# A macaron block with RWKV7 and window attention: attention scores in one plain product each, and four smaller moves of work

## The chip, the cores and the metric

The kernel runs on one core of one Trainium2 chip. The metric is the device time of one execution in microseconds (us), measured in three runs; the median counts. One further execution was recorded by the hardware profiler, and the rows below are from that one.

## The reference, cut to what matters

All arrays are float32; batch 1, 512 rows of 1024 channels, hidden width 2816. Decay, gates and the details of the RWKV7 recurrence are left out here.

```python
h = rms_norm(x, norm_ffn1);  x = x + 0.5 * swiglu(h, gate1, up1, down1)
h = rms_norm(x, norm_mix);   p = h @ w_in            # RWKV columns, and q, k, v of the attention
q, k, v = split(p_attn)                              # 8 query heads, 2 key heads, 64 channels each
o_rwkv = rwkv7_time_mix(p_rwkv)                      # a recurrence over the rows
scores = einsum('bnqhgd,bnkhd->bnhgqk', qb, kb) / 8  # blocks of 128 rows against this and the last block
probs  = softmax(where(band, scores, -inf), with one sink per head)
o_attn = einsum('bnhgqk,bnkhd->bnqhgd', probs, vb)
x = x + concat(o_rwkv, o_attn) @ w_out
h = rms_norm(x, norm_ffn2);  x = x + 0.5 * swiglu(h, gate2, up2, down2)
return rms_norm(x, norm_final)
```

## The kernel before, in words

**Stages.** Feed-forward block a, the projections by w_in, the mixer (RWKV7 and attention together), the product by w_out, feed-forward block b, the last norm. Each large product is done in three passes (mm3w, L681 to L685): both operands are split into a high part that TensorE reads in one pass and the low rest, and high by high, low by high and high by low are summed. ScalarE (ACT) makes the high part of the weights (L160, `hi...`), VectorE (DVE) the low part (L169, `lo...`). The weights come in through SyncE's queue (SP) and GpSimd's (POOL).

**The start.** `start` loads x in two halves of its columns, four tiles of 128 rows each, and the weights of the first pieces, all from SP's queue. Then each row tile's half is turned on TensorE (`start_turn`, `xta`, L536), multiplied by the norm's gain on DVE (`xga`), and split (`AaM`, `AaP`). Turns 0 and 1 come ahead of the first products, turns 2 and 3 inside them, at t = 1 of `plain_step`.

**The feed-forward blocks.** The hidden columns are cut into pieces, which a loop over q takes in order. The first four (`plain_step`) compute 256 hidden columns with plain products into the banks `Pa`, `Pb`; at the end ACT applies Silu (L658, `gta`), DVE multiplies (L659, `gta` again), and for each of four row tiles a `hidden_turn` (TensorE transposes L731 `hta`, ACT copies L732 `hTa`) is put on the list `due` with the q at which it is issued. After that come the pieces of a seven-product scheme (banks X, Y, Q; twelve matmuls each per row pair), whose operands DVE and ACT form and split between them (L547 to L573).

**The mixer.** The RWKV7 part runs over 8 chunks of 64 rows; each is a chain of short steps over all heads (`z` products `pz`, `zd` ACT's copy L1322, `u` products `pu` L1328, state updates `pS`, output). Attention is cut in 8 units, u = 2n + h for query block n and key head h: scores (`sc`), maximum and mask on DVE, exponential on ACT, transposes `pT`, product by V (`av`). A table of step names, ORDER, sets by hand the order in which all of these are issued, so that attention fills TensorE while a chain step is on ACT or DVE. What comes ahead of it, `join` with `beside`, inverts small triangular matrices for RWKV (`px`, `py`, copies `TT`, L1110) while the last projection (`in_ps_av`, attention's v) runs.

**Scores.** Units 0 and 1 (query block 0) use plain float32 products of 64 rows by 128 columns (L1468). For the six others k is split once into `ks` and `kl` (`split_k`) and q by block into `qs` (`split_q`), on ACT and DVE, all of it issued in `beside(0)`; each of four heads j then takes two matmuls of 256 columns, L1471 and L1472.

**The end.** `last_row` scales a row tile by its norm: ACT makes the half k = 0 (L871), DVE the half k = 1 (L873), and SP issues both stores (L874).

Of the kernel before, what the change touches and what calls it, by code (L numbers as in the profile page):

```python
# [5 lines left out]
F32 = mybir.dt.float32  # L6
F32R = mybir.dt.float32r
AF = mybir.ActivationFunctionType
ALU = mybir.AluOpType
AX = mybir.AxisListType  # L10
P = 128
S = 512
# [4 lines left out]
C = 64  # L17
NC = S // C
# [23 lines left out]
OUTW = 4  # L42
# [11 lines left out]
gb.0 ud.2 s.2 w.4.1 m.6.0 o.2 a.2 n.2.0 oe.2 v.3 ah.2 we.4 te.3 n.2.1 z.3 m.6.1 wa.4.0 b.4 ve.3 al.2 sc.5 wd.4.1 zd.3  # L54
w.6.0 u.3 m.5.0 a.3 w.6.1 uv.3 t.4 m.5.1 ah.3 ud.3 s.3 we.6 te.4 al.3 o.3 n.3.0 sc.7 w.5.0 n.3.1 z.4 wa.6.0 m.7.0 b.5
w.5.1 wd.6.1 a.4 m.7.1 zd.4 t.6 oe.3 we.5 ah.4 wd.5.1 w.7.0 u.4 al.4 bp.1 uv.4 te.6 g.1 wd.5.0 w.7.1 bo.1 t.5 ud.4
we.7 s.4 wd.7.0 te.5 o.4 wd.7.1 a.6 oe.4 n.4.0 ge.1 a.5 n.4.1 ah.6 q.1 t.7 al.6 ah.5 b.6 wh.0 gb.1 z.5 al.5 te.7 var.1 ux
wl.0 q.0 a.7 zd.5 var.0 u.5 ah.7 wo.1.0 wh.1 al.7 uv.5 ns.1 s.5 ud.5 wl.1 ht.1 o.5 wo.1.1 n.5.0 oe.5 q.2 n.5.1 z.6 mg.1
b.7 wo.3.0 zd.6 var.2 xa.1 u.6 ns.0 wo.3.1 uv.6 ns.2 ud.6 s.6 xa.3 mh.1 o.6 n.6.0 ht.0 oe.6 ht.2 n.6.1 wo.0.0 mg.2 z.7
mg.0 mh.2 wo.0.1 zd.7 ml.2 mh.0 u.7 ml.1 wh.2 wo.2.0 xa.0 ud.7 wl.2 o.7 wo.2.1 oe.7 ml.0 q.3 wo.5.0 var.3 wh.3 xa.2  # L60
wl.3 wo.5.1 wo.4.0 xa.5 ns.3 wo.7.0 ht.3 wo.4.1 mg.3 wo.7.1 wh.4 xa.4 mh.3 wl.4 wo.6.0 ml.3 wo.6.1 xa.7 xa.6
# [4 lines left out]
KEEP = "rgvaVOe"  # L66
# [116 lines left out]
class Net:  # L183
# [152 lines left out]
    def start(self, x):  # L336

        nc = self.nc
        self.warm()
        self.consts()  # L340
        xin = self.xin = self.new_rows()
        def load(h, *ts):
            for t in ts:
                nc.sync.dma_start(xin[t][:, h * S:h * S + S], x[0, t * P:(t + 1) * P, h * S:h * S + S])
        a = self.a = self.stream("a")
        load(0, 0)
        a.loads(1)
        load(0, 1, 2, 3)
        a.loads(2)
        load(1, 0, 1, 2, 3)  # L350
        a.loads(4)
        self.first_gain()
        self.ss = self.small("ss_a", 8, "ss")
        self.operands_begin("a")
        for t in range(2):
            self.start_turn(t, 0)
            if t == 0:
                a.split(0)

    def start_turn(self, t, h):  # L360
        self.operand_turn(self.xin[t], t, h, self.gain1)
# [61 lines left out]
    def want_high(self, i):  # L423

        name, srcs = self.plan.pop(0)
        raw, n = self.weights_load(name, srcs)
        hi, lo = (self.wp.tile([P, 8, P], F32R, tag="o" + x, name=f"{x}_{name}", bufs=OUTW) for x in ("hi", "lo"))
        self.nc.scalar.activation(hi, raw, AF.Copy)
        self.half = name, raw, hi, lo

    def want_low(self, i):
        name, raw, hi, lo = self.half
# [13 lines left out]
    def weights(self, name, srcs):  # L446

        raw, n = self.weights_load(name, srcs)
        if name.startswith("be"):
            hi, lo = (self.tile4(f"{c}_{name}", (P, 8, P), F32R) for c in ("hi", "lo"))  # L450
        else:
            if name[0] == "o":
                hi, lo = (self.wp.tile([P, 8, P], F32R, tag="o" + x, name=f"{x}_{name}", bufs=OUTW) for x in ("hi", "lo"))
            else:
                hi, lo = (r.next(P) for r in self.split_rings)
        return self.weights_split(raw, n, hi, lo)
# [178 lines left out]
    def plain_step(self, st, pc):  # L635

        nc = self.nc
        if pc.idx == 0:
            self.banks["P"] = [self.acc(f"P{st.tag}{t}") for t in range(4)]
        bh, bl = st.parts[pc.q]  # L640
        for t in range(4):
            if pc.idx == 0 and t == 1 and st.tag == "a":
                for u in (2, 3):
                    self.operand_turn(self.xin[u], u, 0, self.gain1)
                for u in (2, 3):
                    self.operand_split(P_OPERANDS[1][0], u % 2)
            if pc.idx == 0 and t == 2 and st.tag == "b":
                self.out_turn(7)
            hi, lo = self.A[P_OPERANDS[t // 2][pc.idx // 2]]
            ts = slice(t % 2 * P, t % 2 * P + P)  # L650
            for j in range(2):
                k = 2 * (pc.idx % 2) + j
                self.mm3w(self.banks["P"][t], hi[:, k, ts], lo[:, k, ts], bh[:, j], bl[:, j], pc.idx == 0 and j == 0, pc.idx == 3 and j == 1)
        if pc.idx == 3:
            for t, b in enumerate(self.banks.pop("P")):
                ms = self.ms[:, t:t + 1]
                g, h = self.gt(f"pg{st.tag}{t}")[:, :256], self.gt(f"ph{st.tag}{t}")[:, :256]
                nc.scalar.activation(g, b[:, 256:], AF.Silu, scale=ms)  # L658
                nc.vector.scalar_tensor_tensor(h, b[:, :256], ms, g, ALU.mult, ALU.mult)  # L659
                self.due.append((pc.q + 1 + t, lambda t=t, h=h: self.hidden_turn(st, 5, t, h, 256)))  # L660

    def gu_step(self, st, pc):
        nc = self.nc
# [201 lines left out]
    def last_row(self, t):  # L865
        nc = self.nc
        z, o = self.z[t], self.fs[t][:, 2:3]
        for k in range(2):
            hs = slice(k * S, (k + 1) * S)
            if k == 0:  # L870
                nc.scalar.activation(z[:, hs], z[:, hs], AF.Copy, scale=o)  # L871
            else:
                nc.vector.scalar_tensor_tensor(z[:, hs], self.xN[t][:, hs], o, self.nf[:, hs], ALU.mult, ALU.mult)  # L873
            nc.sync.dma_start(self.out[0, t * P:(t + 1) * P, hs], z[:, hs])  # L874

    def finish(self):
        self.last_row(3)
# [138 lines left out]
    def prep(self, p):  # L1016
        nc = self.nc
        k, r, a, Pd, Pi = self.kT[p], self.rT[p], self.icl[p], self.Pd[p], self.Pi[p]
        c3 = lambda t: t.rearrange("p (c t) -> p c t", c=NC)
        KR = self.KR[p] = self.tile4(f"KR{p}", (P, NC, 2, C))  # L1020
        BK = self.BK[p] = self.tile4(f"BK{p}", (P, NC, 2, C))
        STo = self.STo[p] = self.tile4(f"STo{p}", (P, NC, 2, C))
        kk = self.tile2(f"kk{p}")
        kk3 = c3(kk)
        nc.vector.scalar_tensor_tensor(kk, k, self.v("rwkv_k_k", p), self.knb[p].rearrange("p t s -> p (t s)"), ALU.mult, ALU.mult)
# [133 lines left out]
    def gate(self, p):  # L1159

        nc = self.nc
        if p // 2 not in self.g:
            self.g[p // 2] = self.tile4(f"g{p // 2}")
        pt = self.gps[p] = self.psum(f"g_ps{p}")
        nc.tensor.matmul(pt, self.g2[:, p * P:(p + 1) * P], self.gl, start=True, stop=True)

# [7 lines left out]
    def mixer(self):  # L1174
        nc = self.nc
# [54 lines left out]
        with self.tc.manual_schedule(engines=MAN):  # L1230
# [5 lines left out]
            def beside(i):  # L1236
                if i == 0:
                    part(0, 4)
                    self.split_k()
                    for n in range(1, 4):  # L1240
                        self.split_q(n)
                elif i == 1:
                    self.scores_all(0)
                    part(4, 8)
# [176 lines left out]
    def attn_begin(self):  # L1421
        nc = self.nc
        self.amix = self.pairs("am")
        self.sc, self.qs, self.PT, self.pp = {}, {}, {}, {}

    def attn_values(self):
        self.avn = self.psum("avn", (P, 4, P))
# [4 lines left out]
        self.Vn = self.keep("V", "Vn").rearrange("p (n c) -> p n c", n=4)  # L1432
        self.nc.scalar.activation(self.Vn, self.avn, AF.Copy)

    def split_k(self):

        nc = self.nc
        self.ks = self.x4.tile([P, 2, S], F32R, tag="ks", name="ks", bufs=1)
        self.kl = self.tile2("kl", dt=F32R) if "a" not in KEEP else self.t4.tile([P, 2, S], F32R, tag="kl", name="kl", bufs=1)[:, 0]
        for h in range(2):  # L1440
            r, o = (slice(x * 64, x * 64 + 64) for x in (h, 1 - h))
            nc.scalar.activation(self.ks[r, h], self.k[r], AF.Copy)
            nc.vector.tensor_tensor(self.kl[r], self.k[r], self.ks[r, h].bitcast(F32), ALU.subtract)
            nc.gpsimd.dma_start(self.ks[o, h], self.ks[r, h])

    def split_q(self, n):

        nc = self.nc
        qs = self.qs[n] = self.wp.tile([P, 2, 4, P], F32R, tag="qs", name=f"qs{n}", bufs=3)
        for i in range(2):  # L1450
            js = slice(2 * i, 2 * i + 2)
            for h in range(2):
                r, o = (slice(x * 64, x * 64 + 64) for x in (h, 1 - h))
                q, hi = self.q[i][r, :, n * P:(n + 1) * P], qs[r, h, js]
                nc.scalar.activation(hi, q, AF.Copy)
                nc.vector.tensor_tensor(qs[o, h, js], q, hi.bitcast(F32), ALU.subtract)

    def scores(self, u):
        nc = self.nc
        n, h = u // 2, u % 2  # L1460
        r0 = h * 64
        k0 = 0 if n > 0 else P
        W = 2 * P - k0
        pss = self.psum2(f"sc{u}", (P, 4, 2 * P))
        for j in range(4):
            ks = slice((n - 1) * P + k0, (n + 1) * P)
            if n == 0:
                nc.tensor.matmul(pss[:, j, :W], self.q[j // 2][r0:r0 + 64, j % 2, :P], self.k[r0:r0 + 64, ks], start=True, stop=True)  # L1468
            else:
                q = self.qs[n][:, h, j]  # L1470
                nc.tensor.matmul(pss[:, j, :W], q, self.ks[:, h, ks], start=True, stop=False)  # L1471
                nc.tensor.matmul(pss[:, j, :W], q[r0:r0 + 64], self.kl[r0:r0 + 64, ks], start=False, stop=True)  # L1472
        self.sc[u] = (self.extra4("sc", f"scs{u}", (P, 4, 2 * P)), W, pss) + tuple(self.small(f"{x}{u}", 4, x) for x in ("m", "nm", "es", "den"))

    def scores_max(self, u, half):
# [178 lines left out]
```

## Time and profile before

| | us |
|---|---|
| runs | 999.86, 1001.09, 1001.99 (median 1001.09) |
| the profiled execution's own time | 1002.43 |
| its span, first to last instruction | 1000.7 |
| TensorE busy | 976.9 (98%) |
| VectorE busy | 651.7 (65%) |
| ScalarE busy | 502.9 (50%) |
| mean granted clock of TensorE | 0.988 |

The span is 1.73 us shorter than the execution; that rest lies outside what the profile records. A granted clock of 1.00 is 2.4 GHz, 0.50 is 1.2 GHz. Matmuls are recorded with an overlap, so what a step takes is the distance between the starts of two neighbours rather than the duration of one. A float32 product of the plain kind leaves two matmul records, a pass of a split product one. "Unit" below is one of the attention's eight.

### The profile page before, as it was taken

The numbers are of one execution on the slowest core, as the hardware profiler recorded it, in microseconds if no ns is written. First come the engines' busy times: TensorE is split into PE (matmuls) and PEld (weight loads), VectorE is DVE, ScalarE is ACT, GpSimd is POOL, SyncE is SP. The second block draws the span as 40 slices with busy tenths as digits, with TensorE's granted clock in tenths as the row PEclk, the third lists the DMA queues.
The fourth block names the chain that finished last, engine by engine and source line by source line (L and its number), as shares of the span: only waits on it lengthen the run. The fifth ranks groups of instructions, "written<-read, shape, count | busy, mean of one in ns | idle before, by whom it ended". The sixth has DMA issues, their size and how long they took to land.

```text
span 1000.7 us, 12967 instructions
## 1 busy us (share of the span) xinstructions
PE 976.9 (98%) x5041; PEld 794.6 (79%) x5041; DVE 651.7 (65%) x926; ACT 502.9 (50%) x777; POOL 88.5 (9%) x97
## 2 busy tenths in 40 slices
PE   8799999999999999999989999999999999999996
PEld 6688888888888886788876777887888888888885
DVE  5677667677522548699985687668767668753422
ACT  4655546546521327755466664265554654652302
POOL 0110010110000001120010030101010111000001
PEclk9899999999999999999999899999999999999999
DMA  9474855945332044223110253655594584533202
GB/s 316 106 168 113 225 135 122 232 105 182 111 104 84 12 103 140 75 74 73 43 33 23 52 152 132 226 156 147 124 234 110 143 202 97 206 126 115 75 1 84
DMA packets 83621, 124.09 MB, mean 124 GB/s; under 512 B 12772, under 2 KB 33320, under 8 KB 83560
## 3 DMA queue, kind: packets, MB, share of 16 engines
q1 hardware_dynamic: 67048, 89.17, 27.7%
q0 software_dynamic: 13856, 31.46, 15.8%
q10 hardware_dynamic: 2656, 2.63, 0.9%
q8 instruction: 39, 0.64, 0.3%
q14 instruction: 22, 0.18, 0.1%
HBM read 114.60 MB, written 6.29 MB: 121 GB/s over the span
## 4 chain that ended last, share of the span: by engine, by line
PE 85%; DVE 6%; ACT 4%; issue 2%; DMA 1%; POOL 1%; SPq 0%; POOLq 0%; ACTq 0%; DVEq 0%
PE da L685 4%; PE da L683 4%; PE db L685 4%; PE db L683 4%; PE da L684 4%; PE db L684 4%; PE Xa L685 4%; PE Xa L683 4%; PE Xa L684 4%; PE Xb L685 3%; PE Xb L683 3%; PE Xb L684 3%; PE Qb L685 2%; PE Qa L685 2%; PE Qa L683 2%
## 5 line engine op out<-in xcount | busy, mean ns | idle before, releaser
L160 ACT ACTIVATE hib<-rawa1b 128x1024 fp32r<-128x1024 f32 x38 | 40.2, 1057 | 58.4 <-PE db L684 19.4
L683 PE MATMUL da<-hia,dda 128*128 128x512 f32 x176 | 69.3, 394 | 0.0
L683 PE MATMUL db<-hib,ddb 128*128 128x512 f32 x176 | 68.8, 391 | 0.0
L685 PE MATMUL da<-loa,dda 128*128 128x512 f32 x176 | 68.6, 390 | 0.0
L684 PE MATMUL da<-hia,dda 128*128 128x512 f32 x176 | 68.5, 389 | 0.0
L685 PE MATMUL db<-lob,ddb 128*128 128x512 f32 x176 | 68.5, 389 | 0.0
L684 PE MATMUL db<-hib,ddb 128*128 128x512 f32 x176 | 68.5, 389 | 0.0
L160 ACT ACTIVATE hia<-rawa1a 128x1024 fp32r<-128x1024 f32 x38 | 40.1, 1055 | 49.6 <-DMA rawa1a<-in_ffn_gate_dram 17.6
L169 DVE TENSOR_TENSOR lob<-rawa1b,hib 128x1024 fp32r<-128x1024 f32 x38 | 46.4, 1220 | 28.3 <-PE db L685 22.6
L169 DVE TENSOR_TENSOR lob<-rawa0b,hib 128x1024 fp32r<-128x1024 f32 x38 | 46.4, 1220 | 28.3 <-PE db L685 21.7
L683 PE MATMUL Xa<-hia,AaM 128*128 128x512 f32 x160 | 64.0, 400 | 0.0
L685 PE MATMUL Xa<-loa,AaM 128*128 128x512 f32 x160 | 63.1, 395 | 0.9 <-DVE loa L169 0.9
L685 PE MATMUL Xb<-lob,AbM 128*128 128x512 f32 x160 | 62.6, 392 | 1.3 <-DVE lob L169 1.3
L683 PE MATMUL Xb<-hib,AbM 128*128 128x512 f32 x160 | 63.2, 395 | 0.0
L684 PE MATMUL Xa<-hia,AaM 128*128 128x512 f32 x160 | 62.8, 393 | 0.0
L684 PE MATMUL Xb<-hib,AbM 128*128 128x512 f32 x160 | 62.3, 390 | 0.0
L169 DVE TENSOR_TENSOR loa<-rawa0a,hia 128x1024 fp32r<-128x1024 f32 x38 | 46.4, 1220 | 20.9 <-PE da L685 14.6
L169 DVE TENSOR_TENSOR loa<-rawa1a,hia 128x1024 fp32r<-128x1024 f32 x38 | 46.4, 1220 | 15.8 <-PE da L685 8.8
L160 ACT ACTIVATE hib<-rawa0b 128x1024 fp32r<-128x1024 f32 x38 | 40.1, 1057 | 24.5 <-PE db L684 12.1
L160 ACT ACTIVATE hia<-rawa0a 128x1024 fp32r<-128x1024 f32 x38 | 40.1, 1055 | 15.4 <-PE da L684 11.2
L685 PEld LDWEIGHTS da<-loa,dda 128*128 128x128 f32 x176 | 33.0, 188 | 7.0
L685 PEld LDWEIGHTS db<-lob,ddb 128*128 128x128 f32 x176 | 33.0, 188 | 6.9
(460 smaller groups left out, 2527.9 us busy)
## 6 DMA issues: line engine op xcount, KB each, us to landing
rawa0a<-in_w_in_dram SPq DMA_DIRECT2D x16, 512.0 KB
rawa0a<-in_ffn_down_dram SPq DMA_DIRECT2D x11, 512.0 KB
rawa1a<-in_ffn_down_dram SPq DMA_DIRECT2D x11, 512.0 KB
rawa0b<-in_ffn_down_dram SPq DMA_DIRECT2D x11, 512.0 KB
rawa1b<-in_ffn_down_dram SPq DMA_DIRECT2D x11, 512.0 KB
rawba<-in_ffn_up_dram SPq DMA_DIRECT2D x10, 512.0 KB
rawba<-in_ffn_gate_dram SPq DMA_DIRECT2D x10, 512.0 KB
rawa0a<-in_ffn_gate_dram POOLq DMA_DIRECT2D x10, 512.0 KB, 5.9
```

The costliest lines, as they stand in the source:

```text
L160: self.nc.scalar.activation(hi, raw, AF.Copy)
L169: self.nc.vector.tensor_tensor(lo, raw, hi.bitcast(F32), ALU.subtract)
L683: mm(ps, ah, bh, start=first, stop=False, skip_group_check=True)
L684: mm(ps, al, bh, start=False, stop=False, skip_group_check=True)
L685: mm(ps, ah, bl, start=False, stop=last, skip_group_check=True)
```

## The change

It has five parts. (1) The scores of units 2 to 7 become one plain float32 product per head, 64 rows by 256 columns, as units 0 and 1 have with 128; `split_k` and `split_q` go, with 14 ACT copies, 14 DVE subtractions and two DMAs on POOL. (2) At the start, the first piece's weights are issued by ACT, x follows on SP without them, and turn 1 comes behind the first three products. (3) The four hidden turns of the plain pieces come one step of the loop later in both blocks. (4) The stores of the half k = 0 are issued by ACT. (5) The four loads `ux` (POOL, x from its spill) come behind one norm step, `var.0`. Beside these some tiles share one allocation (`KS`, `g`, `ow`), and the g and h of the plain pieces are taken four by four.

```diff
-we.7 s.4 wd.7.0 ... z.5 al.5 te.7 var.1 ux
-wl.0 q.0 a.7 zd.5 var.0 u.5 ah.7 ...
+we.7 s.4 wd.7.0 ... z.5 al.5 te.7 var.1
+wl.0 q.0 a.7 zd.5 var.0 ux u.5 ah.7 ...
         load(0, 0)
-        a.loads(1)
+        a.loads(1, nc.scalar)
         load(0, 1, 2, 3)
...
-        for t in range(2):
-            self.start_turn(t, 0)
-            if t == 0:
-                a.split(0)
+        self.start_turn(0, 0)
+        a.split(0)
...
                 self.mm3w(self.banks["P"][t], hi[:, k, ts], ...)
+                if st.tag == "a" and (pc.idx, t, j) == (0, 0, 0):
+                    self.start_turn(1, 0)
         if pc.idx == 3:
+            g4, h4 = ([self.gt(f"p{x}{st.tag}{t}")[:, :256] for t in range(4)] for x in "gh")
...
-                self.due.append((pc.q + 1 + t, lambda t=t, h=h: self.hidden_turn(st, 5, t, h, 256)))
+                self.due.append((pc.q + 2 + t, lambda t=t, h=h: self.hidden_turn(st, 5, t, h, 256)))
...
-            nc.sync.dma_start(self.out[0, t * P:(t + 1) * P, hs], z[:, hs])
+            (nc.sync if k else nc.scalar).dma_start(self.out[0, t * P:(t + 1) * P, hs], z[:, hs])
...
                 if i == 0:
                     part(0, 4)
-                    self.split_k()
-                    for n in range(1, 4):
-                        self.split_q(n)
...
-            if n == 0:
-                nc.tensor.matmul(pss[:, j, :W], self.q[j // 2][r0:r0 + 64, j % 2, :P], self.k[r0:r0 + 64, ks], start=True, stop=True)
-            else:
-                q = self.qs[n][:, h, j]
-                nc.tensor.matmul(pss[:, j, :W], q, self.ks[:, h, ks], start=True, stop=False)
-                nc.tensor.matmul(pss[:, j, :W], q[r0:r0 + 64], self.kl[r0:r0 + 64, ks], start=False, stop=True)
+            nc.tensor.matmul(pss[:, j, :W], self.q[j // 2][r0:r0 + 64, j % 2, n * P:(n + 1) * P], self.k[r0:r0 + 64, ks], start=True, stop=True)
```

How the order moves, at three places. First TensorE at the start of the program (`xta` are turns of x, `Pa` the bank of the first products); before, then now:

```order
16 L536 MATMUL xta_139<-pack_106,xN_113 128x128 x4
17 L536 MATMUL xta_152<-pack_106,xN_113 128x128 x4
18 L683 MATMUL Pa_170<-hia,AaM_145 128x512
19 L684 MATMUL Pa_170<-hia,AaM_145 128x512
20 L685 MATMUL Pa_170<-loa,AaM_145 128x512
21 L683 MATMUL Pa_170<-hia,AaM_145 128x512
```

```order
16 L538 MATMUL xta_139<-pack_106,xN_113 128x128 x4
17 L688 MATMUL Pa_162<-hia,AaM_145 128x512
18 L689 MATMUL Pa_162<-hia,AaM_145 128x512
19 L690 MATMUL Pa_162<-loa,AaM_145 128x512
20 L538 MATMUL xta_169<-pack_106,xN_113 128x128 x4
21 L688 MATMUL Pa_162<-hia,AaM_145 128x512
```

The second turn of x stood ahead of the first product and stands behind the third.

Next ScalarE where the mixer begins (`ks`, `qs` are the split k and q, `TT<-px` a copy for the small inverses, `held<-in_ps_av` attention's v, `scs` the first exponentials, `pack<-pz` the first chain step's copy); before, then now:

```order
341 L1110 ACTIVATE held<-py 128x256
342 L1442 ACTIVATE ks<-held 64x512 x2
343 L1455 ACTIVATE qs_3684<-q_2361 64x256 x2
...
348 L1455 ACTIVATE qs_3702<-q_2362 64x256 x2
349 L1110 ACTIVATE TT<-px 32x2x8x32 x2
350 L924 ACTIVATE held<-in_ps_av,pack_106 128x512
351 L1491 ACTIVATE scs_3781,den_3785<-scs_3781,nm_3783 128x128 x4
352 L1493 ACTIVATE es_3784<-es_3784 128x4
353 L1322 ACTIVATE pack<-pz_3809 64x256 x2
```

```order
343 L1115 ACTIVATE held<-py 128x256
344 L1115 ACTIVATE TT<-px 32x2x8x32 x2
345 L929 ACTIVATE held<-in_ps_av,pack_106 128x512
346 L1466 ACTIVATE scs_3742,den_3746<-scs_3742,nm_3744 128x128 x4
347 L1468 ACTIVATE es_3745<-es_3745 128x4
348 L1325 ACTIVATE pack<-pz_3770 64x256 x2
```

Fourteen copies are gone from between the copy of `py` and that of `px`.

Last TensorE at the scores of unit 2 in the mixer (`sc`), between a product by V (`av`) and RWKV's next values (`pv`); before, then now:

```order
2072 L1544 MATMUL av_3893<-PT_3874,held 64x256 x2
2073 L1471 MATMUL sc_3898<-ks,qs_3684 128x256
2074 L1472 MATMUL sc_3898<-kl,qs_3684 128x256
2075 L1471 MATMUL sc_3898<-ks,qs_3684 128x256
2076 L1472 MATMUL sc_3898<-kl,qs_3684 128x256
2077 L1471 MATMUL sc_3898<-ks,qs_3684 128x256
2078 L1472 MATMUL sc_3898<-kl,qs_3684 128x256
2079 L1471 MATMUL sc_3898<-ks,qs_3684 128x256
2080 L1472 MATMUL sc_3898<-kl,qs_3684 128x256
2081 L1280 MATMUL pv_3919<-pack,held 128x128 x4
```

```order
2068 L1519 MATMUL av_3854<-PT_3835,held 64x256 x2
2069 L1447 MATMUL sc_3859<-held,q_2361 128x256 x2
2070 L1447 MATMUL sc_3859<-held,q_2362 128x256 x2
2071 L1283 MATMUL pv_3876<-pack,held 128x128 x4
2072 L1320 MATMUL pz_3883<-SU_3578,KS_2831 128x64 x2
```

Eight matmuls of one pass each have become four plain ones of the same 256 columns, in the same place.

## Rows read from the trace of the kernel before

**Rows 1.** TensorE's waits: engine, what waited for what, total us, times, longest.

```profile
PE hta L731 <- DVE gta L659: 4.6, 1, 4.6
PE avn L1429 <- ACT held L924: 1.4, 1, 1.4
PE pu L1328 <- ACT pack L1322: 0.6, 1, 0.6
```

**Rows 2.** Timeline where the mixer begins: start, us, instruction, idle before.

```profile
511.67 1.29 PE L1134 MATMUL px<-TB,held 32*32 32x32 f32 x128 [1.26 <-ACT held L1110]
...
512.94 5.26 ACT L1455 ACTIVATE qs<-q 64x256 fp32r<-64x256 f32 x12
...
516.61 0.39 PE L508 MATMUL in_ps_av<-h_m,loa 128*128 128x512 f32 x1
...
518.22 1.19 ACT L1110 ACTIVATE TT<-px 32x512 f32<-32x512 f32 x2
...
518.34 0.39 PE L1317 MATMUL pz<-SU,STo 128*128 128x64 f32 x2
...
519.43 0.69 ACT L924 ACTIVATE held<-in_ps_av,pack 128x512 f32<-128x512 f32 x1
...
521.97 0.76 ACT L1322 ACTIVATE pack<-pz 64x256 f32<-64x256 f32 x2
```

**Rows 3.** Timeline of TensorE, scores and products like them.

```profile
530.60 0.38 PE L1471 MATMUL sc<-ks,qs 128*128 128x256 f32 x1
...
533.09 1.16 PE L1280 MATMUL pv<-pack,held 128*128 128x128 f32 x8
...
557.05 1.03 PE L1544 MATMUL av<-PT,held 128*64 128x256 f32 x6
558.01 1.16 PE L1280 MATMUL pv<-pack,held 128*128 128x128 f32 x8
559.00 0.33 PE L1317 MATMUL pz<-SU,KR 128*128 128x64 f32 x2
```

**Rows 4.** Stretches: window, us, engines' busy time (x), TensorE's clock, DMA share, GB/s.

```profile
522.20:529.00 6.80, 6.53 (x27) 3.72 (x28) 4.02 (x17) 3.70 (x11) 0.00 (x0) 0.50 0.01 2
...
563.10:566.50 3.40, 3.40 (x27) 2.05 (x27) 2.94 (x13) 1.05 (x6) 0.00 (x0) 0.51 0.00 0
...
573.40:576.80 3.40, 3.40 (x16) 2.16 (x15) 1.96 (x8) 2.68 (x8) 0.00 (x0) 0.50 0.98 308
...
995.90:998.90 3.00, 0.00 (x0) 0.00 (x0) 0.75 (x1) 0.72 (x1) 0.00 (x0) 0.62 0.93 348
```

**Rows 5.** Timeline of TensorE: eight transposes and their neighbours, at either clock.

```profile
544.82 1.04 PE L1523 MATMUL pT<-pack,scs 128*128 128x128 f32 x8
545.78 0.65 PE L1544 MATMUL av<-PT,held 128*64 128x256 f32 x4
...
575.11 1.89 PE L1523 MATMUL pT<-pack,scs 128*128 128x128 f32 x8
576.93 0.68 PE L1328 MATMUL pu<-pack,TT 64*64 64x64 f32 x16
```

**Rows 6.** Timeline of the start: TensorE, VectorE, ScalarE.

```profile
8.31 1.11 PE L536 MATMUL xta<-pack,xN 128*128 128x128 f32 x4 [2.50 <-DMA xN<-in_x_dram]
...
8.19 1.23 DVE L169 TENSOR_TENSOR loa<-rawa0a,hia 128x1024 fp32r<-128x1024 f32 x1 [0.25 <-ACT hia L160]
...
7.11 1.04 ACT L160 ACTIVATE hia<-rawa0a 128x1024 fp32r<-128x1024 f32 x1
```

**Rows 7.** The chain that ended last, at the start and the hidden turns: start, us, what.

```profile
11.99 1.72 PE xta L536 x8
...
61.57 1.15 DVE loa L169
...
62.77 0.50 PE Xa L685
...
674.69 0.27 ACT hTb L732
```

More of the change, by code (lines that the diff above doesn't have):

```diff
@@ L56 @@
 w.5.1 wd.6.1 a.4 m.7.1 zd.4 t.6 oe.3 we.5 ah.4 wd.5.1 w.7.0 u.4 al.4 bp.1 uv.4 te.6 g.1 wd.5.0 w.7.1 bo.1 t.5 ud.4
-we.7 s.4 wd.7.0 te.5 o.4 wd.7.1 a.6 oe.4 n.4.0 ge.1 a.5 n.4.1 ah.6 q.1 t.7 al.6 ah.5 b.6 wh.0 gb.1 z.5 al.5 te.7 var.1 ux
-wl.0 q.0 a.7 zd.5 var.0 u.5 ah.7 wo.1.0 wh.1 al.7 uv.5 ns.1 s.5 ud.5 wl.1 ht.1 o.5 wo.1.1 n.5.0 oe.5 q.2 n.5.1 z.6 mg.1
+we.7 s.4 wd.7.0 te.5 o.4 wd.7.1 a.6 oe.4 n.4.0 ge.1 a.5 n.4.1 ah.6 q.1 t.7 al.6 ah.5 b.6 wh.0 gb.1 z.5 al.5 te.7 var.1
+wl.0 q.0 a.7 zd.5 var.0 ux u.5 ah.7 wo.1.0 wh.1 al.7 uv.5 ns.1 s.5 ud.5 wl.1 ht.1 o.5 wo.1.1 n.5.0 oe.5 q.2 n.5.1 z.6 mg.1
 b.7 wo.3.0 zd.6 var.2 xa.1 u.6 ns.0 wo.3.1 uv.6 ns.2 ud.6 s.6 xa.3 mh.1 o.6 n.6.0 ht.0 oe.6 ht.2 n.6.1 wo.0.0 mg.2 z.7
@@ L426, in want_high, with out_pair @@
         raw, n = self.weights_load(name, srcs)
-        hi, lo = (self.wp.tile([P, 8, P], F32R, tag="o" + x, name=f"{x}_{name}", bufs=OUTW) for x in ("hi", "lo"))
+        hi, lo = self.out_pair(name)
         self.nc.scalar.activation(hi, raw, AF.Copy)
         self.half = name, raw, hi, lo
+    def out_pair(self, name):
+        t = self.wp.tile([P, 2, 8, P], F32R, tag="ow", name="w_" + name, bufs=OUTW)
+        return t[:, 0], t[:, 1]
     def want_low(self, i):
@@ L452, in weights @@
             if name[0] == "o":
-                hi, lo = (self.wp.tile([P, 8, P], F32R, tag="o" + x, name=f"{x}_{name}", bufs=OUTW) for x in ("hi", "lo"))
+                hi, lo = self.out_pair(name)
             else:
@@ L653, in plain_step @@
                 self.mm3w(self.banks["P"][t], hi[:, k, ts], lo[:, k, ts], bh[:, j], bl[:, j], pc.idx == 0 and j == 0, pc.idx == 3 and j == 1)
+                if st.tag == "a" and (pc.idx, t, j) == (0, 0, 0):
+                    self.start_turn(1, 0)
         if pc.idx == 3:
+            g4, h4 = ([self.gt(f"p{x}{st.tag}{t}")[:, :256] for t in range(4)] for x in "gh")
             for t, b in enumerate(self.banks.pop("P")):
                 ms = self.ms[:, t:t + 1]
-                g, h = self.gt(f"pg{st.tag}{t}")[:, :256], self.gt(f"ph{st.tag}{t}")[:, :256]
+                g, h = g4[t], h4[t]
                 nc.scalar.activation(g, b[:, 256:], AF.Silu, scale=ms)
                 nc.vector.scalar_tensor_tensor(h, b[:, :256], ms, g, ALU.mult, ALU.mult)
-                self.due.append((pc.q + 1 + t, lambda t=t, h=h: self.hidden_turn(st, 5, t, h, 256)))
+                self.due.append((pc.q + 2 + t, lambda t=t, h=h: self.hidden_turn(st, 5, t, h, 256)))
     def gu_step(self, st, pc):
@@ L1019, in prep @@
         c3 = lambda t: t.rearrange("p (c t) -> p c t", c=NC)
-        KR = self.KR[p] = self.tile4(f"KR{p}", (P, NC, 2, C))
+        both = self.t8.tile([P, 2, NC, 2, C], F32, tag="KS", name=f"KS{p}", bufs=4)
+        KR, STo = self.KR[p], self.STo[p] = both[:, 0], both[:, 1]
         BK = self.BK[p] = self.tile4(f"BK{p}", (P, NC, 2, C))
-        STo = self.STo[p] = self.tile4(f"STo{p}", (P, NC, 2, C))
         kk = self.tile2(f"kk{p}")
@@ L1161, in gate @@
         nc = self.nc
-        if p // 2 not in self.g:
-            self.g[p // 2] = self.tile4(f"g{p // 2}")
+        if not self.g:
+            both = self.t8.tile([P, 2, 2, S], F32, tag="g", name="g", bufs=1)
+            self.g = {i: both[:, i] for i in range(2)}
         pt = self.gps[p] = self.psum(f"g_ps{p}")
@@ L1423, in attn_begin @@
         self.amix = self.pairs("am")
-        self.sc, self.qs, self.PT, self.pp = {}, {}, {}, {}
+        self.sc, self.PT, self.pp = {}, {}, {}
     def attn_values(self):
@@ L1433, in evac_vn @@
         self.nc.scalar.activation(self.Vn, self.avn, AF.Copy)
[L1435 to L1456, printed above, removed]
     def scores(self, u):
```

## The prediction

> **What bounds the kernel now.** I read the times first, then the list of what TensorE waits for, then the stretches in which the granted clock falls, and last the timelines around these. TensorE is busy for 976.9 of 1000.7 us, so the kernel is bound by TensorE nearly everywhere, and a change is worth something only where it takes away a wait of TensorE, work on TensorE, or time at the lower clock. The list of waits is short [rows 1]: 4.6 us where the first hidden turn waits for VectorE, and where the mixer begins 1.4 us (`avn` for ScalarE's copy `held`) and 0.6 us (`pu` for ScalarE's copy of `pz`). The stretches show three places in the mixer, of 6.8, 3.4 and 3.4 us, at a granted clock of 0.50 or 0.51, the 1.2 GHz level [rows 4]; the first begins right after the two waits. These numbers are from an execution of 1002.43 us, of which 1000.7 are the span; it stands 1.34 us above the median of the runs, so I sum against 1002.43 and take 1.34 off at the end. About 0.2%, or 2.0 us, is what a measurement of this kernel can tell from no change.
>
> **Part 1, the waits at the mixer's start: -2.05 us.** ScalarE goes through twelve `qs` copies from 512.94 on, 5.26 us in all, and the copy `TT` starts only behind them, at 518.22 [rows 2]. `px`, which `TT` reads, was done at 512.96 (511.67 + 1.29), and the projection that `held` copies was done at 517.0 (516.61 + 0.39). So without the `qs` and `ks` copies `TT` runs at 513 to 514.2 and `held` at about 517.05 to 517.75, before the last `pz` ends at about 518.6. The wait of 1.44 behind it goes. ScalarE then does the exponentials that stand between, which took from 520.12 (end of `held`) to 521.97, now from 517.75 or so to 519.6, and `pack` from 519.6 on; `pu` follows `avn` and unit 1's scores, twice four products of 128 columns at some 0.99 us [rows 3], so it comes up at about 520.6, when `pack`, two copies in 0.76, is through or nearly so. So 1.44 + 0.56 and a small gap: 2.05. Bounds: -1.4, if `pu` still waits, and -2.6, if the neighbouring issue gaps shrink too. VectorE loses 14 subtractions with them, which nothing on TensorE waited for.
>
> **Part 1, the products: -3.1 us.** A unit of split scores takes 533.09 - 530.60 = 2.49 us, eight passes of 0.31 [rows 3]. No plain float32 product of 64 rows by 256 columns is in the trace. One bound is that each of its two records takes the 0.31 that a record of 256 columns takes now: then a unit stays at 2.49, and the term is 0. The other is the product by V, 256 columns wide, whose six records take 558.01 - 557.05 = 0.96, 0.16 each; eight make 1.28, and six units save 6 x 1.21 = 7.3. But these have only 64 output channels and lie two abreast, so they flatter. The nearest row is `pv`, four plain products of 128 columns with 128 output channels in 559.00 - 558.01 = 0.99 us; twice the columns is 1.98 a unit, 0.51 less, and for six units -3.1. That I take.
>
> A rule speaks against this part: the Trainium skill, FP8 and Floating Point Precision, section TensorE Precision Notes, says that true FP32 takes four passes through the array, while the reduced form is read truncated; a product with two passes would then be replaced by one with four. By that alone the scores would cost twice what they do. The trace shows that a pass of the split form is not at its column rate (0.31 us for 256 columns, while a plain record of 128 columns takes 0.124), so passes cannot be counted at one price; what the rule would make of the time is the second rival below.
>
> **The clock: -4.2 us.** Eight transposes take 545.78 - 544.82 = 0.96 us at the full clock and 576.93 - 575.11 = 1.82 at half [rows 5], a factor of 1.9. TensorE's busy time in the three stretches is 6.53, 3.40 and 3.40 us [rows 4], of which 1 - 1/1.9 = 0.47 is lost: 3.1, 1.6 and 1.6, in all 6.3. The first stretch begins behind the two waits that part 1 takes away, and I count it fully. The other two follow units of split scores and chain steps without any wait; as the shape of that work changes they may go or move, and I count a third of them, 1.1. Bounds: 0 (every stretch reappears somewhere) and -6.3.
>
> **The chain of the mixer: +0.6 us.** What TensorE saves there can turn into waits for ScalarE or VectorE in the RWKV chain, whose copies get no faster. While attention fills TensorE a chunk takes 12.5 us (two between the `pv` at 533.09 and that at 558.01 [rows 3]), filled without a wait of TensorE; so there is slack, and I allow 0.6 for small new waits; 0 to +6 as bounds. The loads `ux` issued later are four transfers on POOL; their readers on VectorE come behind other work, 0 to +0.3, within this.
>
> **Part 2, the start: +0.8 us.** Now TensorE begins with turn 1 at 8.31, as x lands, and the first product follows 1.11 later [rows 6]. `loa`, which the third product needs, is done at 8.19 + 1.23 = 9.42. The new order can run two products from 8.2 on, must wait for `loa` at 9.42, then does the third, turn 1 (9.88 to 10.95) and the other three at 0.43 each ((11.99 - 9.42) / 6 by [rows 6, 7]), and reaches turns 2 and 3 at about 12.25; now they start at 11.99 [rows 7]. So the order alone loses 0.26. On top, the weights are issued by ScalarE behind its gain load, later than by SP now, and share the transfers' time with three tiles of x. They were there by 7.11, where `hia` starts [rows 6]. If they land only when turn 1's x does now, about 8.3, `hia` and `loa` come 1.2 later, +1.4 in all. I take the middle, +0.8; if they come later still, +3 is the end I keep. The earlier landing of x pays nothing, since turn 1 stands behind products.
>
> **Part 3, the hidden turns: -0.5 + 0.5 us.** The wait of 4.6 us shrinks, since twelve matmuls that need no hidden turn go ahead of it. But the chain that ended last goes on through VectorE and ScalarE up to VectorE's split that ends at 62.72 (61.57 + 1.15), when a product of bank X starts that waited for the last `loa` [rows 7]. VectorE's work up to there is not reduced, so what TensorE gains at the turn it waits again for `loa` later. What leaves the chain is one copy of a hidden turn on ScalarE in each block (0.27 in b [rows 7]; I take the same in a): -0.5. TensorE's new idle time around 50 to 62 us might bring a further stretch at half clock there, which now follows the 4.6: a chance of 0.3 of 1.6 us, +0.5. Bounds: -2.5, if VectorE's order happens to have room, and +2.
>
> **Part 4, the stores: -0.1 us.** ScalarE idles between its scalings at the end, so its issue costs nothing; the last two row tiles' stores move at 348 GB/s with a DMA share of 0.93 from 995.9 to 998.9 [rows 4], so they are limited by the transfer, not the issue. 0 to -0.4.
>
> **Sum.** -2.05 - 3.1 - 4.2 + 0.6 + 0.8 - 0.5 + 0.5 - 0.1 = -8.05. 1002.43 - 8.05 - 1.34 = 993.0 us.
>
> **The rivals.** First, the clock gives nothing back: the half-clock stretches stay or move, since two of the three follow no wait. The rest is -3.85: 997.2. For it speaks that the mixer keeps the same kind of small products; against it that the first stretch follows the two waits directly.
>
> Second, slower: a plain float32 product of 256 columns costs four steps of 0.31 rather than two. Then 24 products cost 0.62 more each, +14.9 in place of -3.1, and the sum is +9.95: 1011.0. From 0.83 us a product on (0.62 now, and 4.95 us of other gains over 24) the change as a whole is slower. Against it: `pv` has 0.2475 a product of 128 columns, and would have to grow 3.3 times for twice the columns.
>
> Third, the mixer's chain takes it all: the RWKV chain on ScalarE and VectorE sets the pace as soon as TensorE is quicker, and the products and the clock only turn into waits. Then -8.05 + 3.1 + 4.2 = -0.75 is left: 1000.3. For it: the chunks with little attention left run at the chain's own pace. Against it: the list of waits has none inside the mixer but the two of [rows 1].
>
> Fourth, the weights at the start come very late: +3 for +0.8, so 995.2.
>
> **How the numbers follow.** The forecast has a chance of 0.57, the clock's rival 0.20, the mixer's 0.12, the late weights 0.06, the slow products 0.05. Faster by more than 0.2% means below 999.1: forecast, clock and late weights, 0.83, and a little of the third, less a little of the clock's: 0.83. Within 0.2%: the rest of the third, 0.11. Slower: 0.06. The forecast's own range is 988 to 997. The low end, 986.5, is the forecast with most of the clock (-2.1 more), scores between `pv` and the product by V (-2 more) and the execution's spread; the high end, 1000, takes in the clock's rival and half of the mixer's.
>
> **What would show it.** In the profile after: no wait of `avn` and at most a trace of one at `pu`; a unit of scores near 2.0 us between its neighbours' starts (2.49 or more refutes the products' term); the stretch at 522 to 529 at full clock; a first product at 8.2 to 9.4 us and the third turn of x at 12.2 to 13.5; the wait of `hta` below 2.5 us and longer waits of X and Y products for `loa`. The prediction is wrong if the mixer, from its first `pz` to the last, is not 8 us or so shorter.

## The result, and the profile after

The changed kernel took 993.92 us (median of four runs, 993.58 to 995.12) against 1000.95 us for the kernel before on the same chip: a ratio of 0.9932, 95% interval 0.9915 to 0.9949. Forecast were 993.0 us. The profiled execution took 993.61 us with a span of 991.9 us, 8.8 us less than before on both counts.

The sum came out; two of its terms did not. TensorE's waits, of the changed kernel (columns as in [rows 1]):

```profile
PE Pa L688 <- ACT hia L160: 5.6, 1, 5.6
PE hta L736 <- DVE gta L664: 1.8, 1, 1.8
...
PE Ya L690 <- DVE loa L169: 1.4, 1, 1.4
...
PE Xa L690 <- DVE loa L169: 1.1, 2, 0.7
```

The waits `avn` and `pu` of [rows 1] are gone, the hidden turn's is 1.8 instead of 4.6, and at its head stands a new one: 5.6 us, in which the first product waits for the first weights (the kernel before waited 2.5 us at the start, for x [rows 6]). The chain that ended last shows why (start, us, what; compare [rows 6, 7]):

```profile
1.86 0.42 ACTq L145
...
2.31 7.66 DMA rawa0a<-in_ffn_gate_dram
...
10.06 1.06 ACT hia L160
...
11.16 0.79 PE Pa L688
```

Issued by ScalarE at 2.31, the second half of these weights needs 7.66 us; `hia` starts at 10.06 rather than 7.11. Where the mixer begins, the kernel before has, beside what [rows 2] shows, its first `pz`:

```profile
516.84 0.33 PE L1317 MATMUL pz<-SU,KR 128*128 128x64 f32 x2
```

The timeline of the changed kernel there:

```profile
515.51 1.19 ACT L1115 ACTIVATE TT<-px 32x512 f32<-32x512 f32 x2 [1.38 <-PE px L1139]
...
519.11 0.39 PE L510 MATMUL in_ps_av<-h_m,loa 128*128 128x512 f32 x1
519.34 1.89 PE L1320 MATMUL pz<-SU,KS 128*128 128x64 f32 x16
519.54 0.69 ACT L929 ACTIVATE held<-in_ps_av,pack 128x512 f32<-128x512 f32 x1 [2.84 <-PE in_ps_av L510]
...
521.07 0.61 PE L1432 MATMUL avn<-pack,held 128*128 128x128 f32 x4
...
521.76 0.76 ACT L1325 ACTIVATE pack<-pz 64x256 f32<-64x256 f32 x2
...
522.69 0.68 PE L1331 MATMUL pu<-pack,TT 64*64 64x64 f32 x16
```

`held` is copied as soon as its projection ends, `avn` and `pu` follow without an idle time. Two of the six units of scores in the same trace, against [rows 3] and [rows 5]:

```profile
527.57 1.99 PE L1447 MATMUL sc<-held,q 64*128 64x256 f32 x8
529.49 1.16 PE L1283 MATMUL pv<-pack,held 128*128 128x128 f32 x8
...
562.07 1.99 PE L1447 MATMUL sc<-held,q 64*128 64x256 f32 x8
563.99 2.00 PE L1320 MATMUL pz<-SU,KS 128*128 128x64 f32 x16
...
566.94 1.09 PE L1498 MATMUL pT<-pack,scs 128*128 128x128 f32 x8
567.96 0.45 PE L1331 MATMUL pu<-pack,TT 64*64 64x64 f32 x8
```

A unit takes 529.49 - 527.57 = 1.92 us instead of 2.49; and the eight transposes that took 1.82 in [rows 5] at half clock take 1.02. The stretches (columns as in [rows 4]):

```profile
8.75:15.50 6.75, 4.30 (x12) 3.00 (x13) 1.92 (x3) 1.69 (x2) 0.00 (x0) 0.50 1.05 363
49.30:52.80 3.50, 3.37 (x8) 2.68 (x9) 3.01 (x4) 3.37 (x5) 0.00 (x0) 0.54 0.00 0
...
522.50:529.30 6.80, 6.80 (x63) 4.63 (x61) 5.08 (x19) 5.14 (x17) 0.00 (x0) 1.00 0.01 2
529.30:567.90 38.60, 38.60 (x322) 29.65 (x320) 28.57 (x105) 30.04 (x91) 0.00 (x0) 1.00 0.12 29
```

All three stretches at 1.2 GHz in the mixer are gone; what is left lies at the start and at 49 us, behind the waits of `hta` and `Ya`. Neither is new in kind. At the start the first passes of the kernel before stood 0.43 us apart as well, up to 13.8 us, against 0.23 behind that. And around the hidden turns the kernel before had a longer stretch:

```profile
40.90:47.70 6.80, 3.54 (x10) 2.87 (x11) 5.15 (x7) 6.77 (x11) 0.00 (x0) 0.50 0.00 0
```

To see where time went, I put the start of the same TensorE instruction in both traces side by side; the difference changes only where time is won or lost. First `pz`: 516.84 and 519.34, so +2.50. `pu`: 522.47 and 522.69, +0.22. First of the six units: 530.60 and 527.57, -3.03. `pu` after the last unit: 576.93 and 567.96, -8.97. Ahead of block b's hidden turns it is still -8.97 (672.75 and 663.78), behind them -9.20 (691.17 and 681.97). These four, before and then now:

```profile
672.75 0.39 PE L685 MATMUL Xb<-lob,AbM 128*128 128x512 f32 x1
...
691.17 0.50 PE L685 MATMUL Xb<-lob,AbM 128*128 128x512 f32 x1 [0.74 <-DVE lob L169]
```

```profile
663.78 0.39 PE L690 MATMUL Xb<-lob,AbM 128*128 128x512 f32 x1
...
681.97 0.50 PE L690 MATMUL Xb<-lob,AbM 128*128 128x512 f32 x1 [0.29 <-DVE lob L169]
```

| term | forecast | measured, profile against profile |
|---|---|---|
| start, and hidden turns in a | +0.8 - 0.25 + 0.5 = +1.05 | +2.5 |
| waits at the mixer's start | -2.05 | -2.3 (2.50 to 0.22) |
| first stretch at 1.2 GHz | -3.1 | -3.2 (0.22 to -3.03) |
| six units of scores | -3.1 | -2.8 (0.58, 0.39, 0.44, 0.39, 0.44, 0.59) |
| the other two stretches | -1.1 | -3.1 (1.50 and 1.62) |
| rest of the mixer up to block b | +0.6 | 0.0 (-8.97 to -8.97) |
| hidden turns in b | -0.25 | -0.25 (-8.97 to -9.22) |
| last stores | -0.1 | +0.4 (-9.2 to -8.8) |
| sum | -8.05 | -8.8 |

The sum is that of the two profiled executions. The medians differ by 7.0 us, since the profiled execution of the kernel before was a long one and that of the changed kernel a short one.

### The profile page after: what moved, and what is told of

It reads as the page before. It is cut to its first block, busy times and chain, and to the rows that moved or that the text cites. A ratio compares the mean times of both kernels' runs of the same rounds, so it can differ in the third digit from the quotient of the medians.

```text
span 991.9 us, 12921 instructions
## 1 busy us (share of the span) xinstructions
PE 967.6 (98%) x5041; PEld 790.1 (80%) x5041; DVE 644.6 (65%) x912; ACT 496.5 (50%) x763; POOL 87.3 (9%) x95
## 4 chain that ended last, share of the span: by engine, by line
PE 86%; DVE 7%; ACT 3%; issue 2%; DMA 1%; POOL 0%; POOLq 0%; ACTq 0%; SPq 0%; DVEq 0%
PE da L690 4%; PE da L688 4%; PE db L688 4%; PE db L689 4%; PE da L689 4%; PE db L690 4%; PE Xb L690 3%; PE Xa L690 3%; PE Xa L688 3%; PE Xb L688 3%; PE Xa L689 3%; PE Xb L689 3%; PE Qb L690 2%; PE Qb L688 2%; PE Qa L690 2%; PE Qa L688 2%
```

## Experiments

All times are beside runs of the kernel before on the same chip, whose medians were 1001.39, 1001.73 and 1000.97 us in the three sets, each on a chip of its own. In brackets stand the ratio to these runs and its 95% interval, or lowest and highest run.

**The start.** Two kernels put parts of it back: the first all of it, the second only the weights' queue.

```diff
-        a.loads(1, nc.scalar)
+        a.loads(1)
...
-        self.start_turn(0, 0)
-        a.split(0)
+        for t in range(2):
+            self.start_turn(t, 0)
+            if t == 0:
+                a.split(0)
...
-                if st.tag == "a" and (pc.idx, t, j) == (0, 0, 0):
-                    self.start_turn(1, 0)
```

The second has the first two lines of this alone.

Expected of the old start: 

> The changed kernel with the start of before: the first weights on SP between the tiles of x, turn 1 of x ahead of the first product. The theory: the start is where the change loses, by weights that land at 9.97 us; with the old order the first product begins at 9.1 again and all that follows moves forward by the +2.5 us which the changed kernel carries into the mixer and some 0.4 that the moved hidden turn had won back: 990.7 to 991.5 us (the changed kernel 993.92). The rival: the delay is hidden behind VectorE's chain up to 65 us anyway, which has its own end; then 993.5 or more.

Expected of the weights on SP: 

> The changed kernel with only the issue of the first weights put back to SP, between the first and second tile of x; turn 1 stays behind three products. The theory (the late weights are the loss, not the moved turn): the first product at about 8.2, the third turn at about 12.25, so +0.3 against the old start, 991.0 to 991.8 us. The rival (the turn behind the products is the loss, since VectorE's part of turn 1 comes later and its chain is the one that ends last): 992.5 to 994.

Measured: 990.12 us (0.9893, 0.9877 to 0.9908) and 990.74 us (0.9898, 0.9883 to 0.9913). Both lie somewhat below what the theories gave, and far from both rivals. In the last set, old start and changed kernel stood side by side:

Expected: 

> The kernel with the old start once more, beside the two others here on the same chip: 990.1 us, as the reference for both.

Expected: 

> The changed kernel once more, beside the one with the old start: the theory has it 3.8 us slower than that, by weights that land late; on another chip or in another run the landing may move, so 3 to 4.5 us.

Measured: 990.14 (989.56 to 990.47) and 993.65 (five of its six runs 993.16 to 994.04, one 997.44). So the start costs the changed kernel 3.5 us side by side (3.8 between sets), and with the weights back on SP all but some 0.6 of it is gone: it is the weights' issue by ScalarE. With the weights on SP the first product runs at 7.75 us, and the third waits 0.36 for `loa`:

```profile
7.75 0.50 PE L688 MATMUL Pa<-hia,AaM 128*128 128x512 f32 x1 [2.39 <-ACT hia L160]
...
9.01 0.80 PE L690 MATMUL Pa<-loa,AaM 128*128 128x512 f32 x1 [0.36 <-DVE loa L169]
```

What the queues moved shows where the time goes. In the changed kernel, from 2 to 4, 4 to 6, 6 to 8 and 8 to 10 us (queue: packets, MB, share of 16 engines; q1 is SP's, q10 ScalarE's):

```profile
q1 hardware_dynamic: 304, 0.56, 85.5%
q10 hardware_dynamic: 16, 0.00, 1.6%
...
q1 hardware_dynamic: 133, 0.24, 39.1%
q10 hardware_dynamic: 129, 0.13, 25.8%
...
q1 hardware_dynamic: 329, 0.43, 59.8%
q10 hardware_dynamic: 304, 0.29, 42.7%
...
q1 hardware_dynamic: 500, 0.63, 90.1%
q10 hardware_dynamic: 111, 0.10, 15.5%
```

SP's queue carries x tiles 1 to 3, the second weights and the other half of x, none of them needed yet. ScalarE's 0.5 MB, issued at 1.86 and 2.31, begin to move only after 4 us (the 16 packets before are the gain load), and from then on they share the engines with SP's. In one queue the weights were ahead of all but the first tile of x. The Trainium skill (DMA: Bandwidth & Descriptors, section Issuing engines are not separate DMA queues) says that transfers from several engines run on the same 16 DMA engines and interleave; the rows agree from 4 us on, both queues being busy in each of these windows. They do not show sharing alone, though: from 2 to 4 us the second queue stands still, and from 4 to 6 us the two together fill 65% of the engines. Why the second queue begins so late stays open. If the second queue gave its transfers a fast lane of their own, these weights would have landed no later than before.

**Queues changed over.** Weights on SP behind the first tile of x, tiles 1 to 3 on ScalarE's queue.

```diff
+        def load(h, *ts, e=nc.sync):
-        load(0, 1, 2, 3)
+        load(0, 1, 2, 3, e=nc.scalar)
```

Expected: 

> The changed kernel with the two queues at the start changed over: the first weights on SP right behind the first tile of x, tiles 1 to 3 of x on ScalarE's queue; turn 1 stays behind three products. The theory (the two queues share the transfer, and what comes in on the second one lands late whatever it is): the weights land before 7 us as in the kernel before, x1 lands at about 10 us or later, turn 1 waits for it instead of the first product for the weights; 991.5 to 993.5 us, between the changed kernel (993.92) and the one with all on SP (990.74). The rival (only the order of bytes counts, weights first is enough): 990.7.

Measured: 991.26 us (990.76 to 991.87; 0.9904, 0.9885 to 0.9924), which is just below what the theory gave and above the rival's 990.7. The theory's own step failed: turn 1 did not wait for x. The time differs little from all on SP (990.74, from another set). So here the loads that are needed later could go to the second queue at little cost, and the urgent one could not.

**Turn 1 one product earlier.** With the weights on SP, turn 1 stands where TensorE waits for `loa`.

```diff
...
         mm(ps, al, bh, start=False, stop=False, skip_group_check=True)
+        if getattr(self, "mid_mm", None):
+            self.mid_mm()
...
```

Expected: 

> The changed kernel with the first weights on SP, and turn 1 of x between the second and the third product instead of behind the third: where TensorE waits for loa anyway (0.36 us there). The theory (the end of the start is set by VectorE's chain over turn 1, which now starts some 0.7 us earlier than with the turn behind the third product and as early as with the old start): 990.0 to 990.3 us, about the old start run beside it. The rival (the products that run earlier count): 0.5 us better than the old start, 989.6.

Measured: 989.73 us (989.22 to 990.64; 0.9891, 0.9872 to 0.991) beside 990.14 for the old start: inconclusive, the ranges overlap. It is the lowest median of all, and like the old start it beats both kernels.

**The scores alone.** The kernel before with part 1 and nothing else (the products as in the change's diff, and `split_k`, `split_q` not called).

Expected: 

> The kernel before with nothing but the plain scores (no split copies, one float32 product per head and unit). The theory: the mixer gains all of what the changed kernel gained there, -2.3 for the two waits, -2.8 for the products, -6.4 for the three stretches at 1.2 GHz, so some -11.2 us: 989.5 to 990.5 us, faster than the changed kernel. The rival: the other parts (KS in one tile, the moved spill loads) have a share of the mixer's gain; then 992 or more.

Measured: 991.08 us (990.09 to 991.55; 0.9902, 0.9884 to 0.992), which lies between the theory's 990.5 and the rival's 992. Part 1 is the whole gain and more: alone it is 10.3 us faster than the kernel before, and the changed kernel, with the new start and the other parts, 7.0. Its mixer, from 514.0 on, runs without a stretch:

```profile
514.00:564.60 50.60, 50.60 (x418) 38.85 (x416) 36.26 (x134) 38.15 (x119) 0.00 (x0) 1.00 0.16 41
```

**What the clock follows.** The next two kernels separate the two things that part 1 takes away. One has the plain products (the change's diff for these alone) but still makes the copies that nothing reads, so that the waits stay. The other has the split products, but the q copies of two blocks stand later, so that the waits go:

```diff
-                    for n in range(1, 4):
-                        self.split_q(n)
+                    self.split_q(1)
...
-a.0 n.0.1 ... z.1 ve.1 al.0 m.2.1 ...
+a.0 n.0.1 ... z.1 ve.1 al.0 sq.2 m.2.1 ...
...
-wa.1.1 w.2.1 ... n.1.0 a.1
+wa.1.1 w.2.1 ... n.1.0 sq.3 a.1
```

(`sq` is `split_q`.)

Expected of the copies kept: 

> The kernel before with the plain scores, but the split copies of q and k are still made (nothing reads them). The theory: the waits for held (1.4) and pack (0.6) stay and with them the stretch at 1.2 GHz behind them, while the two later stretches go with the split products: of the -11.2 us some -2.8 - 3.1 = -5.9 remain, 995 us. The rival A (the split products cause none of the stretches, only the waits do): stretches two and three stay too, -2.8, 998. The rival B (all three stretches go with the split products, the wait has no part): -9.1, 991.9.

Measured: 996.47 us (995.33 to 996.95; 0.9954, 0.9936 to 0.9972). The waits are there, one stretch of half the length follows them, and up to 569.8, where the scores are done, no other:

```profile
PE avn L1429 <- ACT held L924: 1.5, 1, 1.5
...
PE pu L1328 <- ACT pack L1322: 0.9, 1, 0.9
```

```profile
516.00:522.90 6.90, 4.58 (x35) 3.93 (x33) 6.16 (x22) 6.22 (x19) 0.00 (x0) 1.00 0.04 9
522.90:526.30 3.40, 3.34 (x20) 2.00 (x19) 3.05 (x15) 1.42 (x4) 0.00 (x0) 0.50 0.00 0
526.30:569.80 43.50, 43.50 (x362) 33.03 (x360) 30.87 (x110) 33.72 (x104) 0.00 (x0) 1.00 0.19 48
```

The time lies between the theory's 995 and rival A's 998, but the profile is the theory's: the first stretch stays in part, the two others are gone. It is of the fastest of the four runs; the others took 1.0 to 1.6 us longer at a granted clock of 0.991 rather than 0.992, and no trace of them is kept. Beside the scores alone, in the same set, the copies cost 5.4 us.

Expected of the splits later: 

> The kernel before with split scores as they are, but only k and the first block of q are split ahead of the mixer; the q copies of blocks 2 and 3 stand later in the mixer's order (behind al.0 and behind n.1.0). So ScalarE is free for TT and held before TensorE asks for them. The theory (the two waits start the first stretch at 1.2 GHz, split units the two others): the waits of 1.4 and 0.6 go, the first stretch goes or halves, the stretches at 563 and 573 us stay; -2.3 and -1.6 to -3.2, less up to 1 us for copies that now stand between the chain's steps: 996.5 to 998 us beside about 1001. The rival (any stretch comes from the density of the split products): the waits go, all three stretches stay, 998.5 to 999.5. A stretch at 563 or 573 that goes too would refute the theory.

Measured: 1002.56 us (1001.23 to 1004.62; 1.0017, 1.0006 to 1.0029), no gain at all, and outside what either theory gave. The two waits went, and with them the stretch at 522 us. But the copies now stand in the way of the chain: `pv` waits 0.8 and `pz` 1.3 us for VectorE, and two stretches of 6.8 us come later (the first from 547.3 on, inside the window shown).

```profile
PE pz L1316 <- DVE SU L1352: 1.3, 1, 1.3
...
PE pv L1279 <- DVE held L1172: 0.8, 1, 0.8
```

```profile
515.00:546.30 31.30, 29.07 (x219) 21.15 (x217) 23.45 (x82) 23.85 (x73) 0.00 (x0) 1.00 0.09 20
546.30:553.10 6.80, 6.80 (x32) 4.19 (x33) 3.64 (x15) 4.08 (x13) 0.00 (x0) 0.58 0.00 0
...
571.20:578.00 6.80, 6.80 (x43) 5.10 (x42) 3.13 (x14) 3.87 (x11) 0.00 (x0) 0.50 0.65 195
```

The two together: where TensorE waits some 2 us at the mixer's start a stretch follows, with either kind of product; with split products more stretches come, also where no wait precedes (571 us here, 563 and 573 us in [rows 4]); with plain products none came in a mixer without these waits, in any of the ten profiles. That is what the profiled executions show; one run of the changed kernel took 997.44 us at a granted clock of 0.990, where the profiled one beside it had 0.993, and where its further time at 1.2 GHz lay no trace tells. Why a stretch comes behind split products stays open: in this kernel their passes start 0.31 us apart at the full clock and 0.51 at the lower one, so they are not slowed in proportion, but nothing here shows what in them lowers the clock.

**The hidden turns alone.** The kernel before with part 3.

Expected: 

> The kernel before with nothing but the hidden turns of the plain pieces one step later, and the buffers of these taken four by four. The theory: the wait of 4.6 us shrinks below 2.5 and comes back as waits for loa, TensorE gains one copy of ScalarE in each block: -0.5 in a and -0.5 in b, 1000.2 us beside 1001.2. The rival (VectorE has room): -2 or more. The other rival (the moved idle time starts a new stretch at 1.2 GHz where TensorE is on the critical path): 0 or slower.

Measured: 998.34 us (996.75 to 1000.59; 0.9978, 0.9965 to 0.999), more than forecast. But its profile gives the hidden turns only 0.4 us in a and 0.3 in b, by the starts of the same instructions; most of the rest lies in the mixer, where it had two stretches of 3.4 us and the profile of before 6.8, 3.4 and 3.4. These vary between runs of one program with split scores: the kernel before ran from 997.68 to 1002.57 us in the three sets, with a granted clock of 0.990 or more in the runs below 999 us and of 0.988 or 0.989 in the others. Yet 8 of the 11 runs here are below 999 us, and 4 of the 21 of the kernel before beside them; why this kernel has the shorter stretches more often stays open. With plain scores, the scores alone against the next kernel below, which adds parts 3 and 5, gives 991.08 to 990.18; the runs of the two overlap and are from two chips, so this -0.9 only agrees with the profile's -0.7.

**The last stores.** The old start's kernel with all stores on SP.

Expected: 

> The kernel with the old start (990.12 us) and all last stores issued by SP again. In three profiles with ScalarE's issue the span ends 4.5 us after the last scaling, in three with SP's 4.0 to 4.3. The theory: ScalarE's issue lets the last two stores run side by side and end later, so SP's is better by 0.3 to 0.5 us: 989.7. The rival (the end is set by the transfer, or by what lies outside): 990.1, no difference; the forecast on record had ScalarE's issue better by 0.1.

Measured: 990.18 us (989.23 to 990.58; 0.9891, 0.9874 to 0.9908) beside 990.12: no difference, the theory fell. In this profile the span too ends 4.5 us after the last scaling with SP's issue. Which queue issues the stores does not matter here; the +0.4 in the table is not tied to that choice.

**The spill loads.** The old start's kernel with `ux` back in its place.

Expected: 

> The kernel with the old start (990.12 us), and the four loads ux back ahead of var.0 on GpSimd's queue. The theory (their readers come behind other work, no wait depends on them): the same within 0.3 us, 990.1. The rival (the later norm step on GpSimd delays the chain of the mixer): slower by 1 us or more.

Measured: 990.23 us (989.81 to 990.64; 0.9897, 0.9881 to 0.9913) beside 990.14: no difference, as expected.

## Why the prediction was right

- **Waits at the mixer's start:** right in place and size (-2.3 for -2.05). The kernel with the copies kept confirms it: products plain, copies still made, and both waits are there. Nothing took their place in the mixer's chain, for which the forecast allowed 0.6.
- **Products:** right. The 2.0 us a unit taken from twice `pv` was 1.92. A plain product took 1.92 / 4 = 0.48 us, where the pair of split passes took 0.62. The second rival priced four steps at 0.31 us each, and a plain product did not take that. The rule behind it, of the Trainium skill (FP8 and Floating Point Precision, section TensorE Precision Notes), that true FP32 takes four passes, is not refuted: a pass of 512 columns takes 0.23 us here (663.55 to 663.78 in the changed kernel), so four of 256 columns at that rate would be an estimated 0.46, near the 0.48. It is the split pass of 256 columns, at 0.31, that is slower than this rate.
- **Clock:** the first stretch went, as forecast (-3.2 for -3.1); for the other two I counted a third and both went entirely, 2.0 us more. The step that failed is "as the shape of that work changes they may go or move, and I count a third of them": in none of the profiles of plain scores did they move.
- **Start:** the step that failed is "if they land only when turn 1's x does now, about 8.3". They landed at 9.97: I took the time of a transfer in SP's queue, while ScalarE's began to move only after 4 us and then shared the engines. The loss was 2.75 us by the product behind turns 2 and 3 (13.35 to 16.10) and 3.15 once TensorE had also waited 0.2 for `AaP`, for +0.8 in the sum. That is the fourth rival's condition, to which the forecast gave a chance of 0.06; its 995.2 did not come, because the clock gave 2.0 more.
- **Hidden turns:** the mechanism was right. TensorE gained 0.45 in a and 0.25 in b, for 0.25 each, although its wait in a fell by 2.8 us: waits of `Ya` and `Xa` for `loa` took the place. The stretch at 49 us is not the further one that was feared, but stands for the longer one at 41 us. That such a stretch costs nothing here, since TensorE waits for `loa` behind it, two executions of the kernel with the old start show: one has none from 44 to 51 us, the other 6.8 us, and all that follows runs no later for it: the second execution is 0.42 us late ahead of that time and 0.39 us late behind it. In this order:

```profile
44.00:51.00 7.00, 5.60 (x26) 4.29 (x25) 6.47 (x8) 5.30 (x8) 0.00 (x0) 1.00 0.00 0
```

```profile
44.05:50.88 6.83, 5.95 (x16) 4.16 (x16) 6.30 (x8) 5.38 (x8) 0.00 (x0) 0.50 0.00 0
```

- **Stores and spill loads:** nothing, as forecast within what can be told.

Of the signs that were to show it, the waits, the unit of scores, the stretch at 522 us and the hidden turn came as said, and the mixer, from its first `pz` to its last, became 11.5 us shorter, for the 8 or so that were said. The start did not: the first product ran at 11.16 rather than by 9.4, the third turn at 15.15 rather than by 13.5. So the mechanism of part 1 is right, and that the time came within 1 us of 993.0 is luck: two errors of opposite sign, each of about 2 us (the start, 3.15 for 0.8, and the two later stretches, 3.1 for 1.1).

## What to carry to other kernels

Read a wait that stands ahead of a stretch at the lower clock with that stretch: taking the wait away was worth 2.3 us, and the stretch behind it 3.2 more. Within one queue the order of issue kept the urgent load ahead; on a second queue it lost that place and landed some 3 us later, though issued only 0.6 us later. And before moving work into an idle time of TensorE, see which engine's chain ends last behind it: here the idle time went somewhere else, and only what left that chain was won.

## What was not expected of the hardware

A plain float32 product of 64 rows by 256 columns took 0.48 us against 0.62 for a pair of split passes, each of which took 0.31 although a pass of 512 columns elsewhere takes 0.23. And between executions of one program with split scores the time varied by some 4 us, and the shorter runs had the higher granted clock; with plain scores, without the copies and with the first weights on SP, all runs of a kernel lay within 1.5 us.
